# A hybrid decoder layer on one core: the merge formed by token, the rotary tables later, longer runs of matmuls, other first loads, other last sums

## The chip, the cores and the metric

The kernel runs on one NeuronCore of one Trainium2 chip. The metric is the device time of one execution in microseconds; 2056.66 us is the median of three runs before the change. The core's engines are called PE (the matrix engine; its weight loads, PEld, are shown apart), DVE (vector), ACT (scalar), POOL and SP (which here only issues transfers). Transfers are issued from SP's or ACT's queue.

## The reference

One layer on 256 tokens of width 2048, all in float32. Cut to what matters:

```
hn = rmsnorm(x)
q, k, v, g_ret, xr, yr, g_a, g_b = split(hn @ w_in)        # 1024 1024 2048 2048 2048 2048 2048 2048
q, k = rotary(q, positions), rotary(k, positions) * 128**-0.5
ret_out = silu(g_ret) * head_groupnorm(retention(q, k, v))
rnn_out = gelu(yr) * rg_lru(causal_conv(xr))
merged = sigmoid(g_a) * (ret_out @ w_proj_ret) + sigmoid(g_b) * (rnn_out @ w_proj_rnn)
h = x + merged @ w_mix_out
h = h + memory_cross_attention(rmsnorm(h), rmsnorm(mem), ...)   # 4 heads of 512, 256 memory tokens
h = h + (silu(gate) * val) @ w_down                             # gate, val = split(conv(rmsnorm(h) @ w_up)), 2 x 5632
return rmsnorm(h)
```

The `positions` enter only through the rotary tables, the cosine and sine of position times frequency.

## The kernel before

**Split operands.** Every float32 operand of a large product is split in two parts, hi (rounded to the matmul's type) and lo (what is left), and a product is made of three: hi x hi, hi x lo and lo x hi. Activations lie as tiles of 128 features by 512: the 256 tokens' hi beside the 256 tokens' lo (`split_cols` L346, `split_pair` L320). A weight comes in chunks of four row tiles by 512 columns ("raw", 1 MB, three buffers, issued on SP at L192). ACT casts two row tiles at a time to hi (L210; the very first on DVE, L208), DVE subtracts to get lo (L211), into six buffers of each kind. `prefetch` (L182) does this for two chunks ahead. `chunks` (L225) hands them to a gemm one after the other; what was put off with `later(n, fn)` (L221) is issued behind the n-th next chunk, so that its PE steps stand between two chunks of a gemm. On each engine the instructions run in the order that the scheduler of the language gave them; `joined` asks for high priority.

**Two forms of gemm**, each over a block of 512 weight columns and, but for the last FFN part, 16 row tiles in four chunks:

- `gemm_t` (L242): the weights are stationary and the result lies by feature, 128 features by 256 tokens. For each weight tile there is a wide matmul (weight's hi against the activations' hi and lo side by side, 512 columns) and a narrow one (weight's lo against the activations' hi, 256 columns), 64 + 64 in all. Two accumulators of two PSUM banks hold four feature tiles; in each, the columns from 256 on gather the small products, and `joined` (L311) copies them out with ACT (L316) and adds them to the others on DVE (L317). Within a chunk, first one accumulator's pair of feature tiles is done (`pr` 0) and then the other's, each with eight matmuls of one width and then eight of the other (L249 to L258).
- `gemm_n` (L280): the activations are stationary and the weights move, and the result lies by token, 128 tokens by 512 features, twice, in one accumulator. Each row tile takes three matmuls of 512 columns for each half of the tokens (L276 to L278), 96 in all.

Three accumulators of this size go round; `px` has two smaller PSUM tiles for all else (scores, transposes).

**Order of the work.** Q's first block (gemm_t, L410), V's first (gemm_n), K's first (gemm_t), V's second (gemm_n), the two gate blocks, then the same again for the second half of the heads, the retention between the chunks; then xr and yr (gemm_t, four times, with the recurrence, `recur` L604, behind a chunk of the next gemm); then the merge; w_mix_out (gemm_n with `residual`, whose result is turned to features by four transposes at a time, `transposed` L300); the memory attention's k and q (gemm_t), v and o; the FFN in three parts, each with gemm_t for gate and value and gemm_n for the way down (`down` L832).

**The norm's factor and the rotary tables.** hn isn't formed: the gain is put on x when it is split, and the factor of each token follows later. `rms` (L415) squares and sums x by ACT (L421), POOL takes the root (L386). Results by token are scaled by it as a scalar for each partition. For results by feature, `spread_tokens` (L371) puts the factor along the free axis: DVE writes a diagonal (L376), PE multiplies a matrix of ones with it (L377), ACT copies it out as `rsb`. The tables (L443 to L464) are nine DVE steps, two sines on ACT and two products with `rsb`. All of this is issued behind Q's gemm; the scheduler puts L377 behind 28 matmuls of V's first gemm. `rotated` (L468) joins Q's accumulators and multiplies them with the tables.

**The merge** (L667 to L695). For each of four blocks of 512 features and each of the two mixers a gemm_t makes the gate (joined, times `rsb`, then the tanh that stands for the sigmoid), a second one the projection (joined), and DVE forms (tanh + 1) x projection by feature. The rnn side goes first and is kept as `mb`; the retention side is added to it, halved and split at once into the stationary tiles for w_mix_out.

**The end.** The last block of the last down gemm is done in two halves of 128 tokens and two of 256 columns: DVE adds a piece to h (L850), ACT squares and sums it (L851, L725), POOL takes the root, four blocks are scaled (L858 to L865) and stored through SP's queue (L866).

**The start.** ACT issues the load of `pa` (128 columns of parameters by feature, of which the first 16 are the norm's gain), SP those of x by feature ("xt", pairs of tiles, L399) and of the first raw chunk in pieces; the order is in `prefetch`.

Of the kernel before, what the change touches and what calls it, by code (L numbers as in the profile page):

```python
# [9 lines left out]
F32 = mybir.dt.float32  # L10
# [3 lines left out]
ALU = mybir.AluOpType  # L14
AX = mybir.AxisListType

P = 128
# [47 lines left out]
def hybrid_layer(  # L65
# [66 lines left out]
    act.dma_start(out=pa, in_=by_feature[:, 0:P])  # L132
# [49 lines left out]
    def prefetch(n):  # L182
        while len(ahead) < n and taken[0] < len(stream):
# [11 lines left out]
            if first:  # L195
                sp.dma_start(out=cid, in_=consts[:, 0:C_DEC])
                sp.dma_start(out=pb, in_=by_feature[:, P : P + 80])
                sp.dma_start(out=pf.rearrange("p a n -> p (a n)"), in_=by_feature[:, P + 80 :])
# [43 lines left out]
    def gemm_t(w, row, st, nk, col):  # L242
# [4 lines left out]
        for k0, parts in chunks(nk, w, row, col):  # L247
            last = k0 + KC >= nk
            for pr in range(2):  # L249
                if first and k0 == 0:  # L250
                    runs = [[(t, kk, j) for t in (0, 1)] for kk in range(KC) for j in range(2)]
                else:
                    if k0 == 0:
                        phase = 0
                    elif last:
                        phase = 1
                    runs = [[(t, kk, j) for j in range(2) for kk in range(KC)] for t in (phase, 1 - phase)]
                    phase = 1 - phase  # L258
                for t, kk, j in (r for run in runs for r in run):
# [9 lines left out]
                if pr == 0 and not last:  # L269
                    st[(k0 + KC) // 2 + 1]  # L270
# [119 lines left out]
    class Pairs(list):  # L390
# [3 lines left out]
        def load(self, n, eng=None):  # L394
# [36 lines left out]
    spread_tokens(rs0)  # L431
# [10 lines left out]

    TWO_PI = 2.0 * np.pi  # L443
# [4 lines left out]
    cos = cp.tile([P, S], F32, name="cos")  # L448
    sin = cp.tile([P, S], F32, name="sin")
    ang, turns, red = (tmp("rot")[:, 0, :] for _ in range(3))  # L450
    dve.tensor_copy(ang, posi)
    dve.tensor_scalar_mul(ang, ang, invf)
    dve.tensor_scalar(out=turns, in0=ang, scalar1=1.0 / TWO_PI, scalar2=MAGIC, op0=ALU.mult, op1=ALU.add)
    dve.tensor_scalar_add(turns, turns, -MAGIC)
    dve.scalar_tensor_tensor(out=red, in0=turns, scalar=-C1, in1=ang, op0=ALU.mult, op1=ALU.add)
    dve.scalar_tensor_tensor(out=red, in0=turns, scalar=-C2, in1=red, op0=ALU.mult, op1=ALU.add)
    dve.scalar_tensor_tensor(out=red, in0=turns, scalar=-C3, in1=red, op0=ALU.mult, op1=ALU.add)
    dve.tensor_scalar(out=red, in0=red, scalar1=3.1415925, scalar2=-3.1415925, op0=ALU.min, op1=ALU.max)
    act.activation(sin, red, AF.Sin)
    dve.scalar_tensor_tensor(out=ang, in0=red, scalar=-1.0, in1=red, op0=ALU.mult, op1=ALU.max)  # L460
    dve.tensor_scalar(out=ang, in0=ang, scalar1=-1.0, scalar2=float(np.pi / 2), op0=ALU.mult, op1=ALU.add)
    act.activation(cos, ang, AF.Sin)
    dve.scalar_tensor_tensor(out=sin, in0=sin, scalar=sign, in1=rsb, op0=ALU.mult, op1=ALU.mult)
    dve.tensor_tensor(out=cos, in0=cos, in1=rsb, op=ALU.mult)  # L464
# [202 lines left out]
    def gated(c0, w, st, b):  # L667

        sig = []
        for a in gemm_t(w0, 0, xs, NT, c0 + b * BW):  # L670
            z = scaled(a, "gz")
            t = tp.tile([P, 2, S], F32, tag="sig", bufs=4, name=nm("sig"))
            act.activation(t, z, AF.Tanh, scale=0.5)
            sig.append(t)
        res = []
        for pr, a in enumerate(gemm_t(w, 0, st, NT, b * BW)):
            z = joined(a, "pz")
            res.append((sig[pr], z))
        return res
# [259 lines left out]
```

## Time and profile before

| | |
|---|---|
| median of three runs | 2056.66 us (2056.39 to 2058.0) |
| profiled execution | 2058.6 us, span 2056.8 us, granted clock 0.998 |
| PE busy | 2043.5 us, 99% |
| DVE busy | 1336.8 us, 65% |
| ACT busy | 1055.4 us, 51% |
| wide matmuls of gemm_t (L266) | 3712, and as many narrow |
| matmuls of gemm_n (L276, L277, L278) | 1016 at each line, some of 256 columns |
| DMA | 392.32 MB, mean 191 GB/s |

"Busy" counts the time in which an engine has an instruction under way. Matmuls overlap in the pipeline, so the mean duration of one is longer than its step from start to start; the steps are read from the timeline or from the chain. The chain is the work that ended last, followed back from the end; what is on it is what a change must shorten. Times in it count from the start of the span.

### The profile page before, as it was taken

The page shows a single profiled execution, that of the slowest core. Times are in us where ns is not written, and L with a number is a line of the kernel's source. Part 1 is how long each engine was busy: PE and PEld are TensorE (multiplying, and loading weights), DVE is VectorE, ACT ScalarE, POOL GpSimd, SP SyncE. Part 2 cuts the span into 40 slices and gives each one's busy share as a digit, 9 for nine tenths or more (in the row PEclk, how much of TensorE's full clock was granted, in tenths as well). Part 3 has the DMA queues.
Part 4 walks back from the last instruction along what each step waited for, and adds up shares of the span by engine and source line. Part 5 has one row for each costly group of instructions (what it writes and reads, how often), then busy time and mean ns, then how long its engine had stood idle before and what let it go on. Part 6 is the DMA issues. An engine that isn't in the chain of part 4 may idle for free.

```text
span 2056.8 us, 27227 instructions
## 1 busy us (share of the span) xinstructions
PE 2043.5 (99%) x10988; PEld 1771.3 (86%) x10988; DVE 1336.8 (65%) x1682; ACT 1055.4 (51%) x1397; POOL 7.7 (0%) x12
## 2 busy tenths in 40 slices
PE   8999999999999999999999999999999999999998
PEld 7888888888888888888888888888888888888887
DVE  6757658888555555566555555577764777656774
ACT  6545447667444444465444454455543555435553
POOL 0000000000000000000000000000000000000000
PEclk9999999999999999999999999999999999999999
DMA  9554554555655565766555555555655555654663
GB/s 330 199 197 163 186 194 156 192 174 168 205 196 190 168 202 194 249 231 205 172 176 172 177 170 178 184 184 177 208 189 194 181 199 167 214 193 164 203 216 114
DMA packets 200399, 392.32 MB, mean 191 GB/s; under 512 B 6737, under 2 KB 11345, under 8 KB 200273
## 3 DMA queue, kind: packets, MB, share of 16 engines
q1 hardware_dynamic: 199040, 388.42, 56.9%
q10 hardware_dynamic: 1232, 2.16, 0.3%
q8 instruction: 86, 1.41, 0.3%
q14 instruction: 41, 0.33, 0.0%
HBM read 388.46 MB, written 2.10 MB: 190 GB/s over the span
## 4 chain that ended last, share of the span: by engine, by line
PE 97%; DMA 1%; ACT 0%; issue 0%; DVE 0%; SPq 0%; POOL 0%; ACTq 0%; POOLq 0%; DVEq 0%
PE acc L266 61%; PE acc L278 11%; PE acc L277 11%; PE acc L276 11%; PE sm L294 2%; DMA raw<-in_w_in 1%; PE sm L611 1%; PE sm L306 1%; ACT junk L421 0%; ACT hi L210 0%; DVE lo L211 0%; PE sm L778 0%; PE sm L377 0%; SPq L399 0%; SPq L192 0%
## 5 line engine op out<-in xcount | busy, mean ns | idle before, releaser
L211 DVE TENSOR_TENSOR lo<-raw,hi 128x1024 fp32r<-128x1024 f32 (+1 forms) x713 | 854.4, 1221 | 545.8 <-ACT hi L210 485.1
L210 ACT CAST hi<-raw 128x1024 fp32r<-128x1024 f32 x711 | 728.3, 1049 | 713.5 <-PE acc L277 264.5
L266 PE MATMUL acc<-s,hi 128*128 128x512 f32 x3712 | 903.2, 392 | 1.4 <-DVE hi L208 1.3
L266 PEld LDWEIGHTS acc<-s,hi 128*128 128x128 f32 x3712 | 679.0, 189 | 130.4 <-ACT s L350 1.6
L266 PEld LDWEIGHTS acc<-s,lo 128*128 128x128 f32 x3712 | 487.6, 191 | 24.9 <-DVE lo L211 1.6
L266 PE MATMUL acc<-s,lo 128*128 128x256 f32 x3712 | 500.1, 283 | 0.5 <-DVE lo L211 0.5
L276 PE MATMUL acc<-hi,s 128*128 128x512 f32 (+1 forms) x1016 | 392.1, 386 | 0.0
L277 PE MATMUL acc<-hi,s 128*128 128x512 f32 (+1 forms) x1016 | 391.2, 385 | 0.0
L278 PE MATMUL acc<-lo,s 128*128 128x512 f32 (+1 forms) x1016 | 391.2, 385 | 0.0
L277 PEld LDWEIGHTS acc<-hi,s 128*128 128x128 f32 x1016 | 191.4, 188 | 38.0 <-DVE s L328 0.5
L278 PEld LDWEIGHTS acc<-lo,s 128*128 128x128 f32 x1016 | 191.2, 188 | 37.8
L276 PEld LDWEIGHTS acc<-hi,s 128*128 128x128 f32 x1016 | 191.4, 188 | 37.4
L316 ACT COPY c<-acc 128x512 f32<-128x512 f32 x116 | 67.0, 579 | 108.8 <-PE acc L266 108.8
L317 DVE TENSOR_TENSOR uz<-acc,c 128x512 f32<-128x512 f32 x44 | 30.3, 688 | 27.3 <-ACT c L316 27.3
L827 DVE SCALAR_TENSOR_TENSOR fv<-uz,pf,fv 128x255 f32<-128x255 f32 (+1 forms) x88 | 38.5, 480 | 7.8 <-ACT fv L825 7.4
L827 DVE SCALAR_TENSOR_TENSOR fg<-uz,pf,fg 128x255 f32<-128x255 f32 (+1 forms) x88 | 38.5, 480 | 7.8 <-ACT fg L825 7.4
L825 ACT ACTIVATE fg<-uz,pf 128x256 f32<-128x256 f32 x44 | 24.1, 595 | 18.5 <-DVE uz L436 18.5
L825 ACT ACTIVATE fv<-uz,pf 128x256 f32<-128x256 f32 x44 | 24.1, 597 | 16.3 <-DVE uz L436 16.3
L350 ACT ACTIVATE s<-sm,pb 128x256 fp32r<-128x256 f32 x48 | 21.7, 471 | 18.3 <-DVE s L351 18.3
L436 DVE TENSOR_TENSOR uz<-uz,rsb 128x512 f32<-128x512 f32 x44 | 30.3, 689 | 0.7
L725 ACT ACTIVATE junk<-nat 128x512 f32<-128x512 f32 (+1 forms) x26 | 15.4, 593 | 25.1 <-DVE nat L709 11.2
L351 DVE SCALAR_TENSOR_TENSOR s<-sm,pb,s 128x256 fp32r<-128x256 f32 x48 | 22.4, 480 | 5.7 <-ACT s L350 5.7
(166 smaller groups left out, 753.0 us busy)
## 6 DMA issues: line engine op xcount, KB each, us to landing
raw<-in_w_in SPq DMA_DIRECT2D x109, 1024.0 KB, 5.1
raw<-in_ffn_w_up SPq DMA_DIRECT2D x88, 1024.0 KB, 5.1
raw<-in_ffn_w_down SPq DMA_DIRECT2D x44, 1024.0 KB, 5.2
raw<-in_w_proj_rnn SPq DMA_DIRECT2D x16, 1024.0 KB, 5.2
raw<-in_w_proj_ret SPq DMA_DIRECT2D x16, 1024.0 KB, 5.2
raw<-in_w_mix_out SPq DMA_DIRECT2D x16, 1024.0 KB, 5.1
raw<-in_xa_w_k SPq DMA_DIRECT2D x16, 1024.0 KB, 5.1
raw<-in_xa_w_q SPq DMA_DIRECT2D x16, 1024.0 KB, 5.1
```

The source lines that it names most:

```text
L210: act.copy(hi[:, ds], raw[:, cs, :])
L211: dve.tensor_tensor(out=lo[:, ds], in0=raw[:, cs, :], in1=hi[:, ds].bitcast(F32), op=ALU.subtract)
L266: pe.matmul(a, part, sx, start=k == 0 and t == 0, stop=k == nk - 1 and t == 0, skip_group_check=True)
L276: pe.matmul(o, h, hi, start=start, stop=False)
L277: pe.matmul(o, l, hi, start=False, stop=False)
L278: pe.matmul(o, h, lo, start=False, stop=stop)
L294: pe.matmul(o, a, b, start=start and i == 0, stop=stop and i == 2, skip_group_check=True)
L316: act.copy(c, a[:, :, S:BW])
L317: dve.tensor_tensor(out=o, in0=a[:, :, 0:S], in1=c, op=ALU.add)
L436: dve.tensor_tensor(out=z, in0=z, in1=rsb2, op=ALU.mult)
L825: act.activation(y, z[:, j, :], AF.Identity, scale=pf[:, 2, t : t + 1], bias=pf[:, 3, t : t + 1])
L827: dve.scalar_tensor_tensor(out=y[:, s:S], in0=z[:, j, 0 : S - s], scalar=pf[:, 2 - s, t : t + 1], in1=y[:, s:S], op0=ALU.mult, op1=ALU.add,)
```

## The change

Five edits go together.

1. The merge's sixteen gemm_t become gemm_n. Gate and product are formed by token, the tanh reads the accumulator with half the norm's factor as its scale, and the product with the projection reads the accumulator as well. The sum m of both mixers is turned to features by `turn_merged` behind the next gemm's first and second chunk: four transposes each, then the split. Tiles with the tag "sig" become twice as wide and half as many; the attention's `pT` take halves of them.
2. `spread_tokens` and the tables are put off with `later(1, tables)`: they are issued behind the second chunk of V's first gemm.
3. In gemm_t the loops over width and over the accumulator change places: in a chunk all sixteen matmuls of one width come first (both accumulators), then all sixteen of the other. The last chunk keeps the order by accumulator, with the widths in the order narrow, wide, wide, narrow. The very first chunk is as before.
4. `pa` is loaded in two pieces, its first 16 columns first on ACT's queue, the others behind the first raw chunk on SP's; the first xt in two halves, the second on ACT's queue.
5. At the end the square and its sum are one DVE step instead of ACT's, and block 2 of the output is stored through ACT's queue.

```
-    act.dma_start(out=pa, in_=by_feature[:, 0:P])
+    act.dma_start(out=pa[:, 0:16], in_=by_feature[:, 0:16])
...
             if first:
+                sp.dma_start(out=pa[:, 16:P], in_=by_feature[:, 16:P])
                 sp.dma_start(out=cid, in_=consts[:, 0:C_DEC])
...
-            for pr in range(2):
-                if first and k0 == 0:
-                    runs = [[(t, kk, j) for t in (0, 1)] for kk in range(KC) for j in range(2)]
-                else:
-                    if k0 == 0:
-                        phase = 0
-                    elif last:
-                        phase = 1
-                    runs = [[(t, kk, j) for j in range(2) for kk in range(KC)] for t in (phase, 1 - phase)]
-                    phase = 1 - phase
-                for t, kk, j in (r for run in runs for r in run):
+            tiles = [(kk, j) for j in range(2) for kk in range(KC)]
+            if first and k0 == 0:
+                runs = [[(t, pr, kk, j) for t in (0, 1)] for pr in range(2) for kk in range(KC) for j in range(2)]
+            elif last:
+                runs = [[(t, pr, kk, j) for kk, j in tiles] for pr in range(2) for t in (1 - pr, pr)]
+            else:
+                runs = [[(t, pr, kk, j) for pr in range(2) for kk, j in tiles] for t in (phase, 1 - phase)]
+                phase = 1 - phase
+            for i, run in enumerate(runs):
+                for t, pr, kk, j in run:
...
-                if pr == 0 and not last:
+                if i + 1 == len(runs) // 2 and not last:
                     st[(k0 + KC) // 2 + 1]
...
-                (eng or sp).dma_start(out=t, in_=self.src[:, 2 * k2 : 2 * k2 + 2, :])
+                src = self.src[:, 2 * k2 : 2 * k2 + 2, :]
+                if k2 == 0 and self is xs:
+                    sp.dma_start(out=t[:, 0, :], in_=src[:, 0, :])
+                    act.dma_start(out=t[:, 1, :], in_=src[:, 1, :])
+                else:
+                    sp.dma_start(out=t, in_=src)
...
-    spread_tokens(rs0)
...
+    def tables():
+        spread_tokens(rs0)
+        ang, turns, red = (tmp("rot")[:, 0, :] for _ in range(3))
...
+    later(1, tables)
...
-    def gated(c0, w, st, b):
-
-        sig = []
-        for a in gemm_t(w0, 0, xs, NT, c0 + b * BW):
-            z = scaled(a, "gz")
-            t = tp.tile([P, 2, S], F32, tag="sig", bufs=4, name=nm("sig"))
-            act.activation(t, z, AF.Tanh, scale=0.5)
-            sig.append(t)
-        res = []
-        for pr, a in enumerate(gemm_t(w, 0, st, NT, b * BW)):
-            z = joined(a, "pz")
-            res.append((sig[pr], z))
-        return res
+    def gated(c0, w, st, b, o):
+
+        a = gemm_n(w0, 0, xs, NT, c0 + b * BW)
+        t = tp.tile([P, 2, BW], F32, tag="sig", bufs=2, name=nm("sig"))
+        for tt in range(2):
+            act.activation(t[:, tt, :], a[:, tt, :], AF.Tanh, scale=half_rs0[:, tt : tt + 1])
+        z = gemm_n(w, 0, st, NT, b * BW)
+        dve.scalar_tensor_tensor(out=o, in0=t, scalar=1.0, in1=z, op0=ALU.add, op1=ALU.mult)
+        return o
+
+    merged = []
+
+    def turn_merged(m, pr):
+        for t in transposed(m[:, :, pr * S : (pr + 1) * S]):
+            merged.append(split_pair(t, 0.5))
...
+    mb = [gated(O_GB, w_proj_rnn[0], rnn, b, big([P, 2, BW], s="mb")) for b in range(4)]
     for b in range(4):
...
+        m = gated(O_GA, w_proj_ret[0], ret, b, big([P, 2, BW], s="m"))
+        dve.tensor_add(m, m, mb[b])
+        for pr in range(2):
+            later(pr, lambda m=m, pr=pr: turn_merged(m, pr))
...
-                dve.tensor_add(h[:, tt, cs], h[:, tt, cs], accs[c][:, tt, 0:S])
-                square(h[:, tt, cs], ss3[:, tt, b + c : b + c + 1])
+                y = h[:, tt, cs]
+                dve.tensor_add(y, y, accs[c][:, tt, 0:S])
+                junk = tp.tile([P, S], F32, tag="tr", bufs=2, name=nm("junk"))
+                dve.scalar_tensor_tensor(
+                    out=junk, in0=y, scalar=1.0, in1=y, op0=ALU.mult, op1=ALU.mult,
+                    accum_out=ss3[:, tt, b + c : b + c + 1],
+                )
...
-                sp.dma_start(out=out[0, tt * P : (tt + 1) * P, c * BW : (c + 1) * BW], in_=y)
+                queue = act if c == 2 else sp
+                queue.dma_start(out=out[0, tt * P : (tt + 1) * P, c * BW : (c + 1) * BW], in_=y)
```

More of the change, by code (lines that the diff above doesn't have):

```diff
@@ L392, in __init__, with load @@
             self.src, self.wcol, self.raw = src, wcol, []
-        def load(self, n, eng=None):
+        def load(self, n):
             while len(self.raw) < n:
@@ L440, in hybrid_layer @@
     dve.tensor_scalar_mul(half_gn, half_gn, 0.5)
+    cos = cp.tile([P, S], F32, name="cos")
+    sin = cp.tile([P, S], F32, name="sin")
     TWO_PI = 2.0 * np.pi
@@ L447, in hybrid_layer @@
     MAGIC = 12582912.0
[L448 to L461, printed above, removed]
@@ L748, in hybrid_layer @@
     dve.tensor_scalar_mul(lscale, rstd_rows(ss1), float(XD**-0.5))
-    pTs = []
+    pTs, done = [], [0]
     def softmax(q, k):
@@ L778, in transpose_probs @@
                 pe.transpose(t[:, kt, tt * P : (tt + 1) * P], pr_[:, tt, kt * P : (kt + 1) * P], ident)
-        pT = tp.tile([P, 2, S], F32, tag="sig", bufs=4, name=nm("pT"))
+        if done[0] == len(pTs):
+            two = tp.tile([P, 2, BW], F32, tag="sig", bufs=2, name=nm("pT"))
+            pTs.extend(two[:, i, :].rearrange("p (k s) -> p k s", s=S) for i in range(2))
+        pT = pTs[done[0]]
+        done[0] += 1
         act.copy(pT, t)
-        pTs.append(pT)
     for b in range(XH):
```

31 lines of the change are left out of this document (14 added, 17 removed).

## The prediction

> **What bounds the kernel now.** I read the page's busy times first, then the chain that ended last, then the timeline of PE for the price of each kind of gemm, then the start and the end of the span. The busy times and the chain's shares:
>
> ```profile
> PE 2043.5 (99%) x10988; PEld 1771.3 (86%) x10988; DVE 1336.8 (65%) x1682; ACT 1055.4 (51%) x1397; POOL 7.7 (0%) x12
> PE 97%; DMA 1%; ACT 0%; issue 0%; DVE 0%; SPq 0%; POOL 0%; ACTq 0%; POOLq 0%; DVEq 0%
> ```
>
> PE is the chain for 97% of the span. Work removed from DVE or ACT pays only where PE waits for it; a matmul saved pays in full. The timeline of PE inside a gemm_t of the FFN (start, duration, line; rows of equal shape are joined):
>
> ```profile
> 1589.63 3.82 PE L266 MATMUL acc<-s,hi 128*128 128x512 f32 x16
> 1593.29 2.08 PE L266 MATMUL acc<-s,lo 128*128 128x256 f32 x16
> 1595.20 3.82 PE L266 MATMUL acc<-s,hi 128*128 128x512 f32 x16
> ...
> 1600.77 2.00 PE L266 MATMUL acc<-s,hi 128*128 128x512 f32 x8
> 1602.61 1.11 PE L266 MATMUL acc<-s,lo 128*128 128x256 f32 x8
> 1603.56 3.82 PE L266 MATMUL acc<-s,hi 128*128 128x512 f32 x16
> ```
>
> Sixteen wide (512 columns) and sixteen narrow (256) take 1595.20 - 1589.63 = 5.57 us from start to start; one wide is 227 ns and one narrow 120 ns by spacing. A whole gemm_t (64 of each) is 22.29 us: eight follow one another in the chain's piece "PE acc L266 x1024" of 178.29 us. In the chain, gemm_n goes in equal steps of 0.227 us (lines 276, 277, 278), 96 wide ones: 21.76 us; four of them separate two gemm_t starts by 87.1 us. Both stream 49,152 columns. A narrow matmul costs 120 ns and not half of 227, so each matmul has about 13 ns that do not go by its width: 32 fewer of them is 0.43 us, the rest of the 0.53 us is switching between widths.
>
> The chain at the rotary tables (start, duration, piece):
>
> ```profile
> 36.47 2.03 ACT junk L421 x7
> ...
> 38.97 0.71 POOL ro L386
> ...
> 39.78 0.29 DVE diag L376
> ...
> 40.12 0.71 PE sm L377 x4
> 40.83 0.37 PE acc L277
> 41.20 0.43 PE acc L278
> ...
> 44.18 0.29 PE acc L276
> 44.47 0.23 PE acc L277
> ```
>
> And the timeline of PE, whose brackets give the idle time before a row and what released it:
>
> ```profile
> 37.34 0.39 PE L276 MATMUL acc<-hi,s 128*128 128x512 f32 x1
> 40.12 0.71 PE L377 MATMUL sm<-diag,ones 128*128 128x128 f32 x4 [2.38 <-DVE diag L376]
> ```
>
> PE stops inside V's first gemm until the row sums of squares (line 421) give the diagonal; afterwards nine matmuls come 0.43 us apart, half speed, until 44.47. The end:
>
> ```profile
> 2048.97 0.43 DVE nat L850
> 2049.43 0.52 ACT junk L725 x2
> 2050.30 0.59 POOLq L935
> 2050.91 0.72 ACT nat L865
> 2051.64 0.61 ACTq L935
> ```
>
> The last matmul ends at 2048.93; 7.9 us of sums, scaling and stores follow.
>
> **The change part by part.** The sum is made against the profiled execution, 2058.6 us (span 2056.8); the median shown is 2056.66, 1.9 lower, and I shift the result by that.
>
> *Merge formed by token.* Sixteen gemm_t become gemm_n: 16 x (22.29 - 21.76) = **-8.5 us**. Added on PE: 32 transposes, eight groups of four. One such group in a gemm_n, in the chain:
>
> ```profile
> 872.11 0.23 PE acc L278
> 872.34 0.44 PE sm L306 x4
> 872.78 0.23 PE acc L276
> ```
>
> 0.44 to 0.45 us each: **+3.6 us**. They stand at the ends of the next gemm's first two chunks, 5.4 and 10.9 us behind the gemm that made m. Before that come one product (about 1.2 us for 1024 elements by line 211's mean of 1221 ns), one lo that may stand between (1.2) and the sum with mb (1.2): 3.7 us, so PE need not wait; without the 1.7 us of cover it would wait up to 8 x 2 us. The copies (579 ns), joins (688 ns) and rsb products (689 ns) that go are DVE and ACT work that PE did not wait for: 0. The copies of the transposed pair into the stationary tiles are split_pair's as before. PSUM: a gemm_n takes one of three accumulators, so it never waits. SP's loads of x and mem rows come after the last merge gemms' chunks as before, and no raw load queues behind them: 0.
>
> *Runs by width.* In a gemm_t the runs go from w8 n8 w8 n16 w16 n16 w16 n16 w8 n8 w8 to w16 n32 w32 n24 w16 n8 (w wide, n narrow); with the last w8 joined to the next gemm's first, ten runs become six. A gemm_t's own 22.29 is 0.10 us above 64 x 226.7 + 64 x 120 ns, over five wide-narrow pairs, 0.02 us each. Two pairs less in 42 gemm_t: -1.7 us; the rows 5.57 (16+16) against 2 x 2.79 (8+8) give 0.01, so -0.8. I take **-1.5 us**, nearer to whole gemms. It also asks for the second accumulator earlier: after 8 wide (1.84 us) instead of 8 wide and 8 narrow (2.78). It is the buffer whose reading by line 317 ends 1.18 us before the end of the gemm ahead (DVE's row at 1603.43 of 0.69 us, against an end at 1605.29), so 3 us are left; behind the three xr gemms with the recurrence it ends 1.6 us after, and 0.2 to 0.3 us are left. Up to +0.3 x 3 if that cover goes; 0 taken.
>
> *Tables behind V's second chunk.* spread_tokens moves from behind 28 matmuls of V's gemm to behind 48, 10.9 us after its start, about 41.8 us. The diagonal is there at 40.1, from ACT's squares and POOL, which do not move. So the stall and the slow matmuls go: from 37.34 to 44.47 there are ten wide matmuls (2.27) and four small ones (about 0.3 at full speed); 7.13 - 2.57 = **-4.6 us**. But all table steps move too. On DVE they now stand between the lo of K's chunks: the chain of three reductions and the clamp behind lo of K's second chunk, whose raw lands at 48.1; on ACT the sine waits for that and for a table load (1.28 us by the first one), between the hi casts, and then the copies of Q's two accumulators (579 ns, line 316) and their joins follow. Laid out with these durations Q's first accumulator is free at 53.8 us and its second at 56.9. K's gemm, which needs both, would start at 31.2 - 0.3 (first loads, below) + 21.8 + 0.3 (the four small matmuls) = 53.0. Before, it started at 57.69 with both free. New wait: 0.8 us for the first, and after 8 wide (1.84) about 1.3 for the second; **+2.1 us**. Ends: 0 (the copies keep ahead of the table steps) and +4.6 (nothing is gained since ACT and DVE were the limit at 57).
>
> *First loads.* The first matmul is at 6.13, released by the hi cast, which is released by a raw quarter landed at 5.05 behind the scale s (0.48 us on DVE). The cast now goes ahead of it, and pa's first 16 columns instead of 128 go first. That could make the start 0.4 us earlier, but PE then waits for lo of the first chunk's rest (0.53 us idle at 14.85 before), which hangs on landings. The second half of the first xt moves to ACT's queue behind its first table load, at about 2.5 us, instead of 0.74; by the rows of 3 to 4 us to landing it comes at 5.5 to 6, and the matmuls of the second k come after 7. I take **-0.3**, between -0.8 and +0.5.
>
> *Last sums.* One DVE step replaces ACT's square and its readout: from 2049.43 to the rv step at 2049.97 by about 0.3 us less. The last four stores on SP were issued at 2051.66 to 2053.06 and landed until 2055.81; the third goes to ACT's queue, so SP's last issue comes some 0.45 us earlier. **-0.7** (-0.3 to -0.9).
>
> Sum: -8.5 + 3.6 - 1.5 - 4.6 + 2.1 - 0.3 - 0.7 = **-9.9 us**: 2048.7 by the profiled execution, **2046.8** by the median.
>
> [...]
>
> **The rivals.** *A: the tables' delay returns in full at K.* If the second accumulator comes 2 us later than I laid out (one more cast ahead of its copy), or the two new waits slow the clock, the 4.6 + 0.3 us are eaten. For the slow clock: an idle time of 2.38 us was followed by nine slow matmuls (1.6 us), one of 0.53 us by none; the new ones, 0.8 and 1.3, lie between. The sum is then -9.9 + 2.8, 2049.6 by the median; with 1.9 of slow clock on top 2051.5. [...]
>
> *B: a fixed cost that is not per matmul.* If the 0.43 us of a gemm_t is from its reading of the stationary weights (hi and lo) and not from the count, gemm_n would not show 21.76 with the same weights as moving side; the FFN's down gemms have just this form with 0.227 spacing. [...]
>
> *C: slower, by the second accumulator.* Every remaining gemm_t now asks for it 0.94 us earlier. If the reads of lines 316 and 317 come later than 1.84 us after the gemm's end, PE stands in each of 42. Slower than 2060.8 it gets from (9.9 + 4.1) / 42 = 0.33 us each, that is a release 2.2 us after the end where nearly all of them now show 1.18 before: 3.3 us of delay. At 0.5 us each it would be 2068. For it: a lo of 1.2 us may stand ahead on DVE. Against: both engines have less to do.
>
> *D: m late for its transposes.* If a second lo and a hi wait ahead of the sum with mb, 3.7 becomes 5 to 7 us; at 1.5 us for each of the four first groups, and with the clock slow after, +6 to +10: 2053 to 2057. Against: the residual's transposes have the same place and no wait.
>
> **How the numbers follow.** Forecast 0.63 (own range 2044 to 2050), A 0.18, B 0.05, D 0.08, C 0.06. The range takes the unknown bounds: all gains full (tables without new wait, last sums, runs: about 2043.5), and A's far end with the clock and weak runs (2053). A measurement of this kernel tells about 0.2%, 4.1 us, from no change: faster is below 2052.5. That has the forecast, A and half of D (0.85); the same holds B and the other half of D (0.09); slower is C (0.06).
>
> **What the changed profile would show.** Right: L266's count falls by 2048, lines 276 to 278 rise by 512 each, gemm_n steps stay 0.227; eight more groups of transposes with no idle time; no idle time at the diagonal; V to K in 22 us, then idle time at the first and the ninth matmul of K released by the copy and join of Q's accumulators; gemm_t 22.25 us in the FFN; 7.2 us behind the last matmul. Wrong: idle time at the ninth wide matmul of FFN gemms (C), ahead of the merge's transposes (D), or a gemm_n step above 0.23 in the merge (B).

## The result, and the profile after

The changed kernel takes 2052.16 us (median of eleven runs, 2051.7 to 2053.5) against 2057.95 us for the kernel before, eleven runs beside it (2056.3 to 2059.9). The ratio is 0.9974, 95% interval 0.9966 to 0.9983: 5.4 us faster, 3.5 to 7.0 (the two medians lie 5.8 apart). Forecast were 9.9 us. The direction was right, the size forecast was nearly double.

The kernel before has two groups of times, near 2056.4 and near 2058.2 us, with single runs between and above them; the changed one has not. Experiment 8 shows what tells the groups apart: a stretch of some 1.6 us that only the upper one has. The profiled execution of the changed kernel took 2052.15 us, with a span of 2050.4.

The changed kernel's page, busy time of each engine and the shares of its chain:

```profile
PE 2035.5 (99%) x10508; PEld 1745.5 (85%) x10508; DVE 1308.8 (64%) x1630; ACT 1042.7 (51%) x1357; POOL 7.7 (0%) x12
...
PE 79%; DVE 0%; ACT 0%; issue 0%; POOLq 0%; DVEq 0%
```

PE is as full as before, with 480 matmuls less. (The chain reaches back only to 414.83 us, hence the 79%; its other engines are still under 1%.) So the difference must be read from PE's time line, stage by stage. Starts of some gemms in both profiled executions, from the first matmul of each in PE's time line; the third column of numbers is the difference to the changed kernel, the last one takes a later execution of the kernel before, of 2056.34 us (experiment 8):

| start of | before (2058.6) | changed (2052.15) | difference | before (2056.34) | difference |
|---|---|---|---|---|---|
| Q's first gemm | 6.13 | 5.67 | -0.5 | 6.17 | -0.5 |
| V's first gemm | 31.22 | 32.30 | +1.1 | 31.03 | +1.3 |
| K's first gemm | 57.69 | 55.43 | -2.3 | 55.38 | 0.0 |
| V's second gemm | 79.98 | 79.12 | -0.9 | 77.67 | +1.5 |
| first gemm of the merge | 484.65 | 484.16 | -0.5 | 482.34 | +1.8 |
| second gemm of w_mix_out | 866.74 | 861.61 | -5.1 | 864.42 | -2.8 |
| first gemm of the FFN | 1316.47 | 1311.09 | -5.4 | 1314.16 | -3.1 |
| end of the last matmul | 2048.93 | 2042.66 | -6.3 | 2046.60 | -3.9 |
| end of the span | 2056.82 | 2050.36 | -6.5 | 2054.49 | -4.1 |

Nearly all of the gain is made between the start of the merge and the second gemm of w_mix_out: 4.64 us against both. Behind that come another 1.1 us, from the runs by width (experiment 7). What was meant to be gained ahead of 485 us is a loss against the faster execution of the kernel before.

**The merge.** The changed kernel's chain at one of the new groups of transposes (start, duration, piece):

```profile
710.77 0.23 PE acc L278
711.00 0.44 PE sm L306 x4
711.44 0.23 PE acc L276
```

and on DVE and PE the sum m with mb and the transposes that read it:

```profile
708.50 1.22 DVE L695 TENSOR_TENSOR m<-m,mb 128x1024 f32<-128x1024 f32 x1
...
710.84 0.60 PE L306 MATMUL sm<-cid,m 128*128 128x128 f32 x4
```

The sum ends at 709.72, 1.3 us ahead of its transposes, and the row of the transposes has no bracket: PE did not wait. A gemm of the merge takes 21.76 us (GB to its projection, 531.32 to 553.08).

**The runs by width.** PE's time line of a gemm_t in the changed kernel's FFN:

```profile
1577.47 3.79 PE L266 MATMUL acc<-s,hi 128*128 128x512 f32 x16
1581.10 4.00 PE L266 MATMUL acc<-s,lo 128*128 128x256 f32 x32
1584.93 7.44 PE L266 MATMUL acc<-s,hi 128*128 128x512 f32 x32
1592.21 3.04 PE L266 MATMUL acc<-s,lo 128*128 128x256 f32 x24
1595.09 3.82 PE L266 MATMUL acc<-s,hi 128*128 128x512 f32 x16
1598.74 1.11 PE L266 MATMUL acc<-s,lo 128*128 128x256 f32 x8
1599.69 2.68 PE L266 MATMUL acc<-s,hi 128*128 128x512 f32 x11
```

Six runs instead of ten; such a gemm now takes 22.25 us (from 1644.18 to 1666.43, for one) instead of 22.29.

**The tables.** The stall at the diagonal is gone, and PE waits elsewhere. The changed kernel's PE at the end of V's first gemm and the start of K's:

```profile
54.34 0.39 PE L278 MATMUL acc<-lo,s 128*128 128x512 f32 x1
55.43 2.08 PE L266 MATMUL acc<-s,hi 128*128 128x512 f32 x8 [0.70 <-DVE q L317]
58.61 1.62 PE L266 MATMUL acc<-s,hi 128*128 128x512 f32 x6 [1.09 <-DVE q L317]
```

The steps between these starts are 0.87 and 1.26 us longer than without a wait. The releaser is the reading of Q's accumulators, which stands behind the tables' steps: on ACT the copy, two casts and a table load,

```profile
50.71 0.57 ACT L316 COPY c<-acc 128x512 f32<-128x512 f32 x1
51.18 1.05 ACT L211 CAST hi<-raw 128x1024 fp32r<-128x1024 f32 x1
52.25 1.28 ACT L466 ACT_TABLE_LOAD   x1
53.54 0.42 ACT L466 ACTIVATE sin<-rot 128x256 f32<-128x256 f32 x1
```

and on DVE the additions at 54.60 and, behind the first half of the rotation, 57.77:

```profile
54.60 0.68 DVE L317 TENSOR_TENSOR q<-acc,c 128x512 f32<-128x512 f32 x1
55.20 0.41 DVE L471 TENSOR_TENSOR cos<-cos,rsb 128x256 f32<-128x256 f32 x1
55.65 0.69 DVE L484 TENSOR_TENSOR ta<-q,cos 128x512 f32<-128x512 f32 x1
56.35 1.39 DVE L486 TENSOR_TENSOR tb<-q,sin 64x512 f32<-64x512 f32 x2
57.77 0.69 DVE L317 TENSOR_TENSOR q<-acc,c 128x512 f32<-128x512 f32 x1
```

**The first loads.** Q starts earlier and ends later. Two rows of PE in Q's gemm of the changed kernel (s is a split tile of x):

```profile
8.91 0.73 PE L266 MATMUL acc<-s,hi 128*128 128x512 f32 x2 [1.44 <-DVE s L351]
...
14.82 1.19 PE L266 MATMUL acc<-s,hi 128*128 128x512 f32 x4 [1.12 <-ACT hi L211]
```

The first waits for a tile made from the second pair of xt, which landed at 6.68 us where it had landed at 5.71 before. The second waits for the cast of the second chunk, whose raw halves SP issues at 7.55 and 8.74 us where they were issued at 5.93 and 6.75.

**The end.** The changed kernel's last steps:

```profile
2042.70 0.42 DVE L856 TENSOR_TENSOR nat<-nat,acc 128x256 f32<-128x256 f32 x1 [3.05 <-PE acc L278]
2043.16 0.43 DVE L858 SCALAR_TENSOR_TENSOR junk<-nat 128x256 f32<-128x256 f32 x1
2043.51 0.08 DVE L858 DVE_READ_ACCUMULATOR junk<-nat 128x1 f32 x1
2043.63 0.21 DVE L384 TENSOR_SCALAR rv<-ss,pt 128x1 f32<-128x1 f32 x1
```

From the last matmul's end to the step at L384 it is 0.97 us, before 1.04.

### The profile page after: what moved, and what is told of

It is laid out like the page before. It is cut to its first block, busy times and chain, and to the rows that moved or that the text cites. A ratio compares the mean times of both kernels' runs of the same rounds, so it can differ in the third digit from the quotient of the medians.

```text
span 2050.4 us, 26194 instructions
## 1 busy us (share of the span) xinstructions
PE 2035.5 (99%) x10508; PEld 1745.5 (85%) x10508; DVE 1308.8 (64%) x1630; ACT 1042.7 (51%) x1357; POOL 7.7 (0%) x12
## 4 chain that ended last, share of the span: by engine, by line
PE 79%; DVE 0%; ACT 0%; issue 0%; POOLq 0%; DVEq 0%
PE acc L266 35%; PE acc L277 14%; PE acc L276 14%; PE acc L278 14%; PE sm L294 1%; PE sm L306 1%; PE sm L620 0%; DVE xr L637 0%; PE sm L780 0%; ACT hi L211 0%; ACT nat L875 0%; DVE lo L212 0%; ACT c L316 0%; PE sm L377 0%; ACT s L327 0%
## 5 line engine op out<-in xcount | busy, mean ns | idle before, releaser
L266 PE MATMUL acc<-s,hi 128*128 128x512 f32 x2688 | 639.2, 391 | 6.1 <-DVE s L351 2.3
L276 PE MATMUL acc<-hi,s 128*128 128x512 f32 (+1 forms) x1528 | 592.0, 387 | 0.0
L277 PE MATMUL acc<-hi,s 128*128 128x512 f32 (+1 forms) x1528 | 590.0, 386 | 0.0
L278 PE MATMUL acc<-lo,s 128*128 128x512 f32 (+1 forms) x1528 | 590.0, 386 | 0.0
L266 PEld LDWEIGHTS acc<-s,hi 128*128 128x128 f32 x2688 | 496.0, 188 | 106.7 <-DVE s L351 2.9
L266 PEld LDWEIGHTS acc<-s,lo 128*128 128x128 f32 x2688 | 342.4, 191 | 11.6 <-DVE lo L212 0.8
L266 PE MATMUL acc<-s,lo 128*128 128x256 f32 x2688 | 350.5, 283 | 0.0
L278 PEld LDWEIGHTS acc<-lo,s 128*128 128x128 f32 x1528 | 287.1, 188 | 58.2
L277 PEld LDWEIGHTS acc<-hi,s 128*128 128x128 f32 x1528 | 287.2, 188 | 56.9 <-DVE s L328 0.4
L276 PEld LDWEIGHTS acc<-hi,s 128*128 128x128 f32 x1528 | 287.2, 188 | 56.5
L316 ACT COPY c<-acc 128x512 f32<-128x512 f32 x84 | 48.4, 578 | 112.1 <-PE acc L266 112.1
L327 ACT ACTIVATE s<-fo 128x512 fp32r<-128x512 f32 x22 | 13.9, 631 | 26.6 <-DVE fo L901 26.6
```

Of the source, the lines that this page charges most:

```text
L266: pe.matmul(a, part, sx, start=k == 0 and t == 0, stop=k == nk - 1 and t == 0, skip_group_check=True)
L276: pe.matmul(o, h, hi, start=start, stop=False)
L277: pe.matmul(o, l, hi, start=False, stop=False)
L278: pe.matmul(o, h, lo, start=False, stop=stop)
L316: act.copy(c, a[:, :, S:BW])
```

## The experiments

**1. The first loads as before.**

```
-    act.dma_start(out=pa[:, 0:16], in_=by_feature[:, 0:16])
+    act.dma_start(out=pa, in_=by_feature[:, 0:P])
-                sp.dma_start(out=pa[:, 16:P], in_=by_feature[:, 16:P])
...
-                if k2 == 0 and self is xs:
-                    sp.dma_start(out=t[:, 0, :], in_=src[:, 0, :])
-                    act.dma_start(out=t[:, 1, :], in_=src[:, 1, :])
-                else:
-                    sp.dma_start(out=t, in_=src)
+                sp.dma_start(out=t, in_=self.src[:, 2 * k2 : 2 * k2 + 2, :])
```

> The changed kernel with the first loads as they were (one transfer for pa, one for the first xt). Ring theory (transfers of SP and ACT take eight semaphores in turn, and each waits until the one eight before it has landed; two transfers more push the raw loads of Q's second chunk to later partners): these two raw loads are issued at about 5.9 and 6.8 us again instead of 7.55 and 8.74, and V's first gemm starts at 31.2 us or a little before (changed kernel 32.30). Rival, that the other order of the casts or the tables made V's start late: it stays at 32.3. End of the last matmul: 1 us earlier than the changed kernel's 2042.7 if the waits at K's start come earlier by as much, no change if they stay.

Measured: the halves are issued at 6.04 and 6.93, V starts at 30.44, the last matmul ends at 2041.31, and six runs have a median of 2050.94 us (ratio to the kernel before 0.9969, 0.9957 to 0.9981). The waits at K's start are 1.5 and 1.25 us: most of the earlier start was kept all the same. In the traces the last matmul ends 1.35 us earlier than in the changed kernel. By the times this part is not shown to cost as much: the median is 1.2 us lower than the changed kernel's, but the two intervals against the kernel before overlap. A gain from it is not seen.

**2. The same bytes and splits in fewer transfers.** pa's rest, pb and pf lie side by side in memory and become one tile and one transfer.

```
-    pa = cp.tile([P, P], F32, name="pa")
-    pb = cp.tile([P, 80], F32, name="pb")
-    pf = cp.tile([P, 4, NF2], F32, name="pf")
+    pg = cp.tile([P, 16], F32, name="pg")
+    pall = cp.tile([P, 192 + 4 * NF2], F32, name="pall")
+    pa = pall[:, 0:112]
+    pb = pall[:, 112:192]
+    pf = pall[:, 192:].rearrange("p (a n) -> p a n", n=NF2)
...
+                sp.dma_start(out=pall, in_=by_feature[:, 16:])
```

> The changed kernel with pa's rest, pb and pf as one transfer of the same bytes into one tile, so that the number of transfers ahead of the second chunk is that of the kernel before, and both splits (pa's first 16 columns, xt's halves) stay. Ring theory: the raw loads of Q's second chunk are issued at 5.7 to 7 us and V starts at 30.7 to 31.2. Rival, that the bytes or the halves of xt are what delays: V starts at 32.3 as in the changed kernel.

**3. One split less.** The first xt whole (as in experiment 1), pa still in two.

> The changed kernel with the first xt whole, pa still in two: one transfer more than before instead of two. Ring theory: the two raw loads of Q's second chunk are issued at about 6.8 and 8.8 us, V starts between 31.2 and 32.3, near 31.7. Rival, the half of xt on ACT's queue as the only cause: V starts at 31.2 or before.

Measured, with the other executions of each kind beside them (the two raw halves are those of Q's second chunk; landings are read from their semaphores):

| transfers ahead, against the kernel before | halves issued at | second half landed | V starts |
|---|---|---|---|
| none more: the kernel before, profiled four times | 5.92 to 6.08, 6.69 to 6.97 | 13.80, 13.22, 13.79, 13.62 | 31.22, 30.64, 31.20, 31.03 |
| none more: experiments 1, 2, 4 | 6.04, 5.84, 6.41; 6.93, 6.26, 6.99 | 13.23, 13.66, 13.99 | 30.44, 30.88, 31.42 |
| one more: experiment 3 | 6.43; 8.26 | 13.29 | 31.52 |
| two more: the changed kernel | 7.55; 8.74 | 15.10 | 32.30 |
| two more: experiments 5, 6, 7, 9 | 7.28, 6.60, 7.26, 7.47; 8.69, 8.03, 8.45, 8.70 | 14.46, 13.86, 14.50, 15.16 | 31.79, 31.07, 31.87, 32.35 |

SP's queue in the changed kernel,

```profile
6.70 0.80 SPq L404 DMA_DIRECT2D xt<-in_x_t  x2
7.55 1.57 SPq L192 DMA_DIRECT2D raw<-in_w_in  x2
```

and in experiment 2:

```profile
5.10 0.33 SPq L404 DMA_DIRECT2D xt<-in_x_t  x1
5.84 1.24 SPq L194 DMA_DIRECT2D raw<-in_w_in  x2
```

In the program each transfer of SP and ACT waits on one of eight semaphores in turn, that of the transfer eight before it; in the traces the ninth and later of these first transfers wait on just these. In the changed kernel the second half is issued at 8.74, right behind the landing of a half of the first chunk at 8.72; before it was issued at 6.75, behind a raw piece landed at 6.73. Experiment 2 keeps both splits and moves the same bytes, with two transfers less, and gets V's start back in its profile: it is the number of transfers and not the splits or the bytes. V's start varies by some 0.5 us about its mean from one execution to the next, so the size is a mean over executions: 31.0 us without additional transfers (seven), 31.9 with two (five), 0.9 us later; the landing is 1.0 us later (13.6 and 14.6). V starts 17.2 to 17.4 us behind that landing in every profile but one, whenever Q's first matmul came (5.67 to 6.60): so an earlier first matmul brought V no nearer. The exception is experiment 3. Its second half landed at 13.29, no later than without additional transfers, and V's start at 31.52 has another wait of PE in it, 0.61 us at 20.77 for lo of a later chunk; that single profile met the forecast for V's start, but not through a later landing. Experiment 2's time is 2051.57 us (0.9970, 0.9958 to 0.9982), experiment 3's single one 2051.75.

**4. The merge alone**, in the kernel before.

> The kernel before with the merge by token alone. Theory, matmuls counted by their steps: each of the sixteen gemms 0.53 us shorter and 32 transposes of 0.11 us more with no idle time ahead of them, so that from the start of the merge to the second w_mix_out gemm 4.6 to 4.9 us are saved, all before and behind it unchanged: last matmul at 2044.2, time 4.7 us under the kernel before. Rival, that part of the merge's gain comes from the runs ahead of it: 3.5 us or less.

Measured: 4.45 us from the start of the merge to the second gemm of w_mix_out, no idle time ahead of the transposes. The last matmul ended at 2042.62 and not at 2044.2, though: in this execution 1.83 us had been saved by the second V gemm, where the kernel is unchanged. Experiment 8 settles that. Ten runs: 2053.34 us (0.998, 0.997 to 0.999), in two groups, 2051.7 to 2052.4 and 2053.3 to 2054.8.

**5. The tables as before.**

```
-    later(1, tables)
+    tables()
```

> The changed kernel with spread_tokens and the tables issued behind Q's gemm again. Theory: PE waits about 2.1 to 2.5 us for the diagonal again, and the two waits at the start of K's first gemm (0.87 and 1.26 us in the changed kernel) go, because Q's accumulators are read in time. So V's gemm grows by 2 to 2.5 us (or by 4.6 where the slow clock follows the wait) and K's is 22.3 us instead of 23.7: last matmul 0 to 0.5 us later than the changed kernel's 2042.7 without the slow clock, 2 us later with it. Rival, the tables' move is worth what I forecast, 2.5 us, in most executions: median 2054.5.

Measured: PE waits for the diagonal again, and the first wait at K's start is gone:

```profile
40.76 0.71 PE L377 MATMUL sm<-diag,ones 128*128 128x128 f32 x4 [1.07 <-DVE diag L376]
...
55.41 1.98 PE L266 MATMUL acc<-s,hi 128*128 128x512 f32 x8
57.91 2.08 PE L266 MATMUL acc<-s,hi 128*128 128x512 f32 x8 [0.53 <-DVE q L317]
```

From V's first gemm to V's second it is 46.63 us, in the changed kernel 46.82. Median 2051.99 us (0.9970, 0.9960 to 0.9981), the changed kernel's 2052.16: the move of the tables is worth nothing here. (The scheduler put L377 six matmuls later than in the kernel before, so the wait was 1.2 us and not 2, and the second wait at K's start stayed with 0.7 us by the steps. It is not quite the old place of the tables, therefore.)

**6. Q's accumulators read early.** The tables stay behind V's second chunk, but the two copies and additions are issued right behind Q's gemm, into a tile of their own.

```
     qacc = gemm_t(w0, 0, xs, NT, O_Q)
+    q0 = big([P, 4, S], s="q0")
+    for pr in range(2):
+        o_ = q0[:, 2 * pr : 2 * pr + 2, :]
+        c_ = tmp("c")
+        act.copy(c_, qacc[pr][:, :, S:BW])
+        dve.tensor_tensor(out=o_, in0=qacc[pr][:, :, 0:S], in1=c_, op=ALU.add)
...
-            q = joined(a[pr], "q")
+            q = made[:, 2 * pr : 2 * pr + 2, :] if made is not None else joined(a[pr], "q")
```

> The changed kernel, but Q's two accumulators are copied out and added right behind Q's gemm into a tile of their own, so that they do not wait behind the tables' steps. Theory: the waits of 0.87 and 1.26 us at K's start go; V's start stays at 32.3, K starts at 54.5 and its gemm takes 22.3 us: last matmul 2.1 us earlier, 2040.5, time about 2050. Rival: the waits are for something else at that place (the raw chunks or their casts): they stay, 2052.

Measured: the additions end at 35.99 and 36.59, K starts without a wait, from V to V it is 44.69 us instead of 46.82. Median 2049.67 us (0.9961, 0.9947 to 0.9975); all five runs lie below all eleven of the changed kernel. The wait was for the accumulators, and only with it gone does the move of the tables pay.

**7. The runs as before.**

> The changed kernel with the runs of matmuls as before. Theory: each gemm_t of the FFN and of the memory attention takes 22.29 us again instead of 22.25 (30 of them, 1.2 us), while the waits of about 0.33 us behind the first eight matmuls of three yr gemms go (0.9 us): last matmul 0.3 to 0.8 us later than the changed kernel's, time the same within 1 us. Rival, that longer runs were worth 1.5 us in all: 1.5 us later.

Measured: from the second gemm of w_mix_out to the last matmul 1.10 us longer than the changed kernel, for 30 gemm_t: 0.037 us each, as forecast. Ahead of it the old order is as good as the new one: from V to V it takes 46.22 us instead of 46.82, because K's second accumulator, free at 58.5 to 58.6 us in both, is asked for later, so that eight narrow matmuls (0.96 us) are done before PE waits for it. The waits in the yr gemms go too, but the xr gemms ahead of them take 26.0 us again where the new order had brought two of them to 25.7, and from V's second gemm to the merge it is 404.97 us, in the changed kernel 405.04. Such a wait in the changed kernel (the third yr gemm):

```profile
413.07 2.00 PE L266 MATMUL acc<-s,hi 128*128 128x512 f32 x8
414.91 0.28 PE L266 MATMUL acc<-s,lo 128*128 128x256 f32 x1
415.36 2.08 PE L266 MATMUL acc<-s,hi 128*128 128x512 f32 x8 [0.18 <-ACT c L316]
```

One narrow matmul stands where the scheduler could put it, then PE waits for the copy of the accumulator of the xr gemm, 0.33 us beyond the usual step. The last matmul ended 0.16 us later than in the changed kernel, the median is 2052.32 us (0.9975, 0.9965 to 0.9986): of the 1.5 us forecast for the runs, hardly anything is left in the sum.

**8. The kernel before, three times more**, for its two groups of times.

> The kernel before once more, for its profile. Its times fall into two groups, near 2056.4 and near 2058.2. Theory: they differ by the slow matmuls behind the wait for the diagonal. If this execution's time is near 2056.4, the matmuls after the four of line 377 come 0.23 us apart at once and K starts near 56; if it is near 2058.2, nine of them come 0.43 us apart and K starts near 57.7. Rival: the difference lies elsewhere in the span.

> The kernel before a third time, for a profile from the lower group of its times (near 2056.4). If this one falls there: no matmuls at 0.43 us behind the wait for the diagonal, and V's second gemm starts near 78 us instead of 80. If it falls in the upper group, near 2058.3: nine of them, as in the two profiles before.

> The kernel before a fourth time, again for a profile from the lower group of its times. Near 2056.4: no stretch of matmuls at 0.43 us behind the wait for the diagonal, the second V gemm starts at 78 to 78.5 us. Near 2058.3: seven to nine such matmuls, second V at 79.5 to 80.2.

The first came out at 2058.8, with 3.20 us of idle time ahead of the diagonal's matmuls and matmuls at 0.43 us behind them until 44.0; the second at 2058.06, the third at 2056.34. PE in the second,

```profile
39.57 0.71 PE L377 MATMUL sm<-diag,ones 128*128 128x128 f32 x4 [1.86 <-DVE diag L376]
40.04 0.48 PE L277 MATMUL acc<-hi,s 128*128 128x512 f32 x1
40.35 0.40 PE L278 MATMUL acc<-lo,s 128*128 128x512 f32 x1
...
41.13 0.63 PE L278 MATMUL acc<-lo,s 128*128 128x512 f32 x1
41.55 0.63 PE L276 MATMUL acc<-hi,s 128*128 128x512 f32 x1
41.98 0.63 PE L277 MATMUL acc<-hi,s 128*128 128x512 f32 x1
```

and in the third:

```profile
39.40 0.71 PE L377 MATMUL sm<-diag,ones 128*128 128x128 f32 x4 [1.85 <-DVE diag L376]
39.86 0.47 PE L277 MATMUL acc<-hi,s 128*128 128x512 f32 x1
40.18 0.39 PE L278 MATMUL acc<-lo,s 128*128 128x512 f32 x1
...
40.87 0.39 PE L278 MATMUL acc<-lo,s 128*128 128x512 f32 x1
41.09 0.40 PE L276 MATMUL acc<-hi,s 128*128 128x512 f32 x1
...
55.16 0.39 PE L278 MATMUL acc<-lo,s 128*128 128x512 f32 x1
55.38 1.98 PE L266 MATMUL acc<-s,hi 128*128 128x512 f32 x8
```

The last two rows are the start of K's gemm: with the tables in their old place PE did not wait there. At the diagonal the idle time is the same, 1.86 and 1.85 us, but in one the matmuls go to half speed 1.4 us after PE resumes and in the other they don't. From V to V it is 48.28 and 46.64 us, a difference of 1.64; the two executions' times differ by 1.72. The traces' records of the granted clock say the same: 0.5 from 40.77 to 44.18 us in the profile of 2058.6, from 40.72 to 44.14 in that of 2058.8, from 40.96 to 44.38 in that of 2058.06, and 1.0 there in that of 2056.34. So the two groups are, by these four profiles, executions with and without the slow clock behind this wait. Experiment 4's profile, with 1.92 us of idle time and no slow matmuls (46.73 us from V to V), is of the second kind too.

**9. The last sums and stores as before.**

> The changed kernel with the last sums on ACT and all last stores on SP's queue as before. What I forecast for these two edits, 0.7 us: from the end of the last matmul to the end of the span 8.4 us instead of 7.7. Theory after the changed kernel's profile: the root starts 0.07 us later and the last store lands by the rate at which the four stores are moved (0.26 MB each at about 380 GB/s, 2.75 us), whatever queue issues them: 7.8 to 7.9 us.

Measured, in one execution of 2052.65 us: 7.81 us from the last matmul to the end of the span, in the changed kernel 7.70. With four issues on SP the last one is at 2047.19, 4.1 us behind the last matmul, and lands 2.8 us later; in the changed kernel it is issued 3.6 us behind and lands 3.2 us later. The four stores moved at 367 to 392 GB/s from the first to the last in the changed kernel; 1.05 MB at 380 GB/s is 2.75 us. From the first issue to the last landing it is 4.20 us on one queue and 4.13 on two: the queue was not what limited them.

**10. A version that takes what was learned**: one transfer less than in the kernel before ahead of the second chunk (pa's gain columns small, all other parameters in one transfer, the first xt whole), Q's accumulators read early, and in the yr gemms the first chunk by accumulator:

```
+            elif late and k0 == 0:
+                runs = [[(t, pr, kk, j) for kk, j in tiles] for pr in range(2) for t in (0, 1)]
+                phase = 1
...
-        for pr, a in enumerate(gemm_t(w0, 0, xs, NT, O_YR + b * BW)):
+        for pr, a in enumerate(gemm_t(w0, 0, xs, NT, O_YR + b * BW, late=True)):
```

> The changed kernel with three things taken together: pa's gain columns in a small transfer of their own, the other parameters by feature in one transfer, the first xt whole (one transfer less ahead of the second chunk than in the kernel before); Q's accumulators added right behind Q's gemm; and in the yr gemms the first chunk by accumulator again. Theory: V starts at 30.5 to 31.2, K's gemm has no waits (44.7 us from V's start to the second V), the waits in the yr gemms go (0.9 us): last matmul near 2038, time 2047.5, 9 to 10 us under the kernel before. Rival, that the wait moves on to the next place (K's end, the rotation, the second accumulators of V): 2049 to 2050 as the early joins alone.

Measured: 2047.33 us, five runs between 2047.26 and 2047.65; ratio to the kernel before 0.9950, 0.9936 to 0.9963. V starts at 31.01, from V to V it is 44.49 us, the last matmul ends at 2037.70. Between V's second gemm and the merge 1.35 us are saved against the changed kernel, 1.17 of them in the last three yr gemms (22.26 to 22.27 us each instead of 22.60 to 22.69). Its PE at K's start:

```profile
53.05 0.39 PE L281 MATMUL acc<-lo,s 128*128 128x512 f32 x1
53.28 3.79 PE L269 MATMUL acc<-s,hi 128*128 128x512 f32 x16
```

## Why the prediction was right and wrong

Two steps failed: the price of the tables' stall, as soon as the sum was taken off the median, and the sign of the first loads. Which of them weighs more depends on the execution that one compares with. Against the profiled execution of 2058.6 us, 9.9 were forecast and 6.5 came in the span; of these 3.4 us the first loads are 1.4, the runs 0.7, the tables 0.6 (forecast -2.5, measured -1.9), the end 0.5 and the merge 0.3. Against an execution near the median of 2056.66, from which the forecast time was taken, the tables are the largest part.

*Merge formed by token: right.* Forecast -8.5 + 3.6 = -4.9; measured -4.64 in the changed kernel and -4.45 alone. The steps of 22.29, 21.76 and 0.44 us carried it. Rivals B and D fell: the gemms take 21.76 us, no run shows the cost that B's chance stood for, and no transposes waited. The 4.5 to 4.6 us saved agree with the fixed part of 13 ns a matmul, an estimate from the spacings (two narrow ones at 120 ns against a wide one at 227).

*Runs by width: right by the gemm, too large in the sum.* 0.04 us a gemm_t came out. The waits for the second accumulator in the yr gemms, which the text bounded at 0.3 x 3 and put at 0, came: 0.3 to 0.4 us in each of three, 1.17 in all by version 10, which takes them away. They and the earlier request in K's gemm (experiment 7) ate most of what the 30 gemms behind the merge gave. C as a rival was this mechanism; beyond K's gemm it stayed confined to three gemms.

*Tables: the step that failed.* That "the stall and the slow matmuls go", 4.6 us, was read from the one profile, and then the sum was taken off the median by a shift of 1.9 us. The 1.9 were not a common offset: they were for the most part the slow clock itself, 1.6 us, which that execution had and the executions near the median of 2056.66 had not. Against an execution without it there were 2.0 us to gain at the diagonal (37.15 to 39.40 in experiment 8), and the new waits at K's start, forecast at 0.8 and 1.3 us and measured at 0.87 and 1.26, took them all: 46.64 us from V to V before, 46.82 after (46.9 to 47.5 in experiments 1, 2, 3 and 9, which have the same tables and runs). In executions with the slow clock the gain is 1.5 to 2.8 us (48.28, 48.76 and 49.59 against 46.82). Rival A's headline, "the tables' delay returns in full at K", describes what came, with a price of 2049.6 by the median; its conditions do not. The second accumulator was not 2 us later than laid out against PE, and the new waits did not slow the clock: they cost what the forecast said, and it was the stall set against them that was too large. That they came out so well has some luck in it. V started 1.4 us later than laid out, and so PE was ready for K at 54.57 instead of 53.0, and the first accumulator was free only at 55.4 instead of 53.8; the two delays cancel in the wait.

*First loads: wrong in sign.* Forecast -0.3 between -0.8 and +0.5; V starts 0.9 us later in the mean, 1.1 in the profiled pair. The prediction counted when each load is issued by its place, and not that each issue waits for the landing of the one eight before (8.74 us, behind a landing at 8.72). The second half of the first xt was issued at 1.25 us, ahead of where it was laid out (2.5). The first matmul did come 0.46 us earlier, but V's start goes by the landing of Q's second chunk, 17.2 to 17.4 us before it in every profile but experiment 3's.

*Last sums: mis-sized.* Forecast -0.7, measured -0.1 to -0.2. DVE's step and its readout take 0.47 us from 2043.16 to 2043.63, where ACT's took 0.54; and issuing the last store 0.5 us nearer to the last matmul brought its landing only 0.1 us nearer, with the stores moving at about 380 GB/s.

Against the execution of 2056.34: forecast -9.9, measured -4.1 in the span. Of the 5.8 between them, tables are 2.7 (forecast -2.5, measured +0.2), first loads 1.6, the runs ahead of the merge and their waits about 0.8, the end 0.5, the merge 0.3; the runs behind the merge gave 0.1 more than their part. What V's start owes to chance in one execution (some 0.4 us here) is in the first loads' share.

## What to carry to other kernels

A stall that is moved off the chain is worth nothing until what stood behind it is moved too: here the accumulators of the gemm before were read behind the tables, and reading them first turned a change that gave 0 into 2 us (from V to V 46.63 us with the tables in their old place, 46.82 with them moved, 44.69 with the accumulators read first). A profile is one execution: where the times shown have a spread, find the stretch that makes it before you subtract, since a term that only some executions have can't be taken from the median. Splitting two loads to get their first bytes early cost those behind them their places in the queue, and V started 0.9 us later in the mean; putting neighbouring small loads into one transfer gave the places back (experiment 2, V at 30.88).

## What was not expected of the hardware

Whether the clock falls behind a wait of PE of this length differs from one execution to the next: 1.85 and 1.92 us of idle time were followed by full speed, 1.86, 2.38 and 3.20 us by six to nine matmuls at 0.43 us, and in the case of 1.86 us that set in only 1.4 us after PE had resumed (39.57 and 40.96). The changed kernel's two waits of 0.70 and 1.09 us, and 1.44 us in Q's gemm, were followed by no such stretch.

By the records of the granted clock the three slow stretches last 3.41 to 3.42 us, whatever the idle time was. In these executions the clock had first risen to full at 10.05, 10.00 and 10.24 us, each 30.72 us before its fall, which is nine times 3.41; experiment 4's execution switches at 5.11, 8.53 and 11.94. Behind the last matmul the clock falls at 2051.22 us in the profile of 2058.6 and at 2046.02 in the changed kernel's, where it had first risen at 4.84: in both 2041.17 us after the first rise, 598 times 3.413. An estimate from these numbers: the switches lie on steps of 3.41 us, which begin at another moment in each execution. Laid on from the first rise, the steps put 1.86, 2.38 and 3.0 us of the idle time at the diagonal into one step where the clock fell behind it, and at most 1.8 (experiment 8's third, first rise at 5.21) and 1.3 us (experiment 4) where it did not. Five executions fit; that this is the cause, no run here shows. The first rise varies much: in seven of the fourteen profiles it came at 9.6 to 10.5 us, in the others at 4.6 to 5.4, so that the first microseconds of Q's gemm ran at half speed in one half of them (in the profile of 2058.6 from a wide matmul's start to the next matmul 0.43 us, at 7.41, and 0.24 behind the rise, at 10.47). V's start does not show it.

Version 10 has the smallest spread of all, 0.4 us over five runs, against 3.6 over the nine of the kernel before beside it. That it has no wait at the diagonal or at K isn't the whole reason: experiment 6 has none either, and its five runs spread over 2.0 us. What else narrows it stays open.
